# The modulation's products on VectorE alone, and layer 2's moved from the two input projections into the first FFN

## The chip, the cores and the metric

One core of one Trainium2 chip runs the kernel as one program. The metric is the device time of one execution in microseconds (us), lower is better. A run's time is compared by the median of several executions.

The engines that matter here are TensorE (PE), VectorE (DVE), ScalarE (ACT), GpSimd (POOL) and SyncE (SP), which issues most of the transfers. Each engine takes its instructions strictly in order, so an instruction that waits also holds up whatever stands behind it on the same engine.

## What is computed

Two layers of a hybrid backbone over 1024 latent and 128 context tokens, width 1024, everything in fp32:

```
for l in range(2):
    sh1, sc1, g1, sh2, sc2, g2 = split(silu(c) @ w_mod[l] + b_mod[l], 6)   # once for c, once for c_ctx
    u = rms_norm(x, norm1_g[l]) * (1 + sc1) + sh1
    mix = mixers(u @ w_in[l] + b_in[l])          # attention, gated DeltaNet, mLSTM
    x = x + g1 * (mix @ w_out[l])
    u = rms_norm(x, norm2_g[l]) * (1 + sc2) + sh2
    x = x + g2 * ((silu(u @ w_gate) * (u @ w_up)) @ w_down)
y = rms_norm(x, final_norm_g)
```

The change concerns the first line alone, the **modulation**: a vector of 1024 numbers (for each of two conditions) times a matrix of 1024 x 6144 per layer. The result is 48 blocks of 128 numbers per layer and condition. `sh1`, `sc1` and `g1` of a layer are needed around its mixers, `sh2`, `sc2` and `g2` around its FFN.

## The kernel before

Tokens lie along the free dimension in three groups of 384 (`GW`); features lie on the partitions in 8 blocks. Each fp32 product on PE is made of three matmuls with parts of the operands (`mm3`, lines 189 to 191): the weights are split by ACT (`wh`, line 183) and by DVE (`wl`, line 184).

A layer goes through these stages: `begin` and `w_in` (the input projection with the preparation of the mixers), `mixers` (recurrences and attention, then half 1 of the output projection), half 0 of `w_out`, the norm, and `ffn`. The emitted order is not the order in which engines run: a list scheduler puts each engine's instructions into a fixed order before the launch, and pools of buffers with a given number of copies (`bufs`) decide how far a producer may run ahead.

Blocks 0 to 15 of layer 1's modulation are made on PE at the very start (`adaln`). The other 80 are made by `ada`, while the input projections run: 32 of layer 1 and the first 16 of layer 2 in layer 1's `w_in`, the other 32 of layer 2 in layer 2's `w_in`. `ada_open` first loads the condition vectors onto every partition (`csb`, 1 MB) and lets ACT take the silu. For each block, 128 rows of the transposed weights (`aw`, 128 x 1024, 512 KB, 5 buffers) come in through SP's queue, and there are two ways to the sum of products along a row:

- condition 0 on DVE (line 240): one instruction multiplies and sums (`aj`), followed by a short readout of the accumulator;
- condition 1 on POOL and ACT: POOL multiplies (`ap`, line 243, 2 buffers), ACT sums (line 244).

In `w_in` up to 6 blocks of modulation are emitted behind each of the projection's blocks `b` from `LATE` = 1 on. The projection's own blocks need all engines too: `blk_b` (lines 700 to 716) multiplies on PE, moves the result out with ACT (`cv`, line 700) and convolves it on DVE (lines 704 to 708); `blk_c` (line 726) and `blk_a` (lines 912 to 952) do likewise.

In `ffn` one hidden block is a `gu` (two products `pg` and `pu`, 48 matmuls for each of three groups), after which DVE multiplies (`hs`, line 370) and splits (`hl`, line 203). Two hidden blocks then go through `dn`: 24 products `pd` of 6 matmuls, each added into `x` by DVE (`add_gated`, line 347). The banks `pg`, `pu` and `pd` have two buffers each in PSUM, and so has `st`, which only the norm uses.

## Time and profile before

| what | value |
|---|---|
| time, three runs | 3957.68, 3957.76 and 3968.36 us, median 3957.76 us |
| span of the profiled execution | 3963.4 us |
| its own time beside the span | not given apart; the span lies 5.6 us over the median |
| PE busy, share of the span | 3587.5 us, 91% |
| DVE busy | 2333.4 us, 59% |
| ACT busy | 1223.3 us, 31% |
| POOL busy | 904.9 us, 23% |
| mean granted clock of PE | 0.939 |

Busy shares are means over stages that differ. In the FFNs PE is busy all the time at its full clock and DVE about four tenths; in the input projections DVE is the fuller engine and PE has gaps. So the change has to be read stage by stage: layer 1's input projection lies within the first 640 us, the first FFN starts near 1200 us, and layer 2 starts near 2030 us.

### The profile page before, as it was taken

The page shows a single profiled execution, that of the slowest core. Times are in us where ns is not written, and L with a number is a line of the kernel's source. Part 1 is how long each engine was busy: PE and PEld are TensorE (multiplying, and loading weights), DVE is VectorE, ACT ScalarE, POOL GpSimd, SP SyncE. Part 2 cuts the span into 40 slices and gives each one's busy share as a digit, 9 for nine tenths or more (in the row PEclk, how much of TensorE's full clock was granted, in tenths as well). Part 3 has the DMA queues.
Part 4 walks back from the last instruction along what each step waited for, and adds up shares of the span by engine and source line. Part 5 has one row for each costly group of instructions (what it writes and reads, how often), then busy time and mean ns, then how long its engine had stood idle before and what let it go on. Part 6 is the DMA issues. An engine that isn't in the chain of part 4 may idle for free. (4 is left out here: it accounts for less than half of the span.)

```text
span 3963.4 us, 59219 instructions
## 1 busy us (share of the span) xinstructions
PE 3587.5 (91%) x22770; PEld 3417.7 (86%) x22770; DVE 2333.4 (59%) x5009; ACT 1223.3 (31%) x2544; POOL 904.9 (23%) x983
## 2 busy tenths in 40 slices
PE   7876888888899999999988798988889999999998
PEld 6876777788789999999987777878779999999997
DVE  7898575768654333333378957656785533433335
ACT  5343322535533111111143442233463411111111
POOL 2276340246310000000023735013551200000001
PEclk8988997899899999999998899979999999999999
DMA  5355743485411111111133575248652111111111
GB/s 206 129 197 165 241 159 111 118 242 155 149 54 38 38 49 43 38 43 43 40 121 135 192 246 182 90 114 246 175 160 68 38 43 38 44 47 38 38 49 59
DMA packets 270177, 434.11 MB, mean 110 GB/s; under 512 B 23880, under 2 KB 185736, under 8 KB 269640
## 3 DMA queue, kind: packets, MB, share of 16 engines
q1 hardware_dynamic: 240664, 324.28, 26.1%
q10 hardware_dynamic: 29232, 106.05, 8.4%
q8 instruction: 180, 2.95, 0.3%
q14 instruction: 101, 0.83, 0.1%
HBM read 315.85 MB, written 114.39 MB: 109 GB/s over the span
## 5 line engine op out<-in xcount | busy, mean ns | idle before, releaser
L347 DVE SCALAR_TENSOR_TENSOR x<-pd,mod,x 128x256 f32<-128x256 f32 (+1 forms) x832 | 404.1, 513 | 667.9 <-PE pd L191 667.2
L183 ACT CAST wh<-wr 128x1024 fp32r<-128x1024 f32 (+1 forms) x219 | 228.6, 1045 | 831.2 <-PE pu L190 457.6
L284 POOL TENSOR_TENSOR nacc<-nacc,nsq 128x384 f32<-128x384 f32 x48 | 52.0, 1083 | 1758.0 <-ACT nsq L283 1750.8
L189 PE MATMUL dn<-uh,wh 128*128 128x384 f32 x864 | 312.9, 362 | 82.7 <-ACT gw L726 37.7
L184 DVE TENSOR_TENSOR wl<-wr,wh 128x1024 fp32r<-128x1024 f32 (+1 forms) x219 | 279.9, 1287 | 164.1 <-ACT wh L183 163.6
L189 PE MATMUL pd<-hh,wh 128*128 128x384 f32 x1056 | 359.6, 341 | 6.9 <-DVE x L347 5.1
L190 PE MATMUL pg<-ul,wh 128*128 128x384 f32 x1056 | 357.9, 339 | 1.8 <-DVE ul L332 1.8
L189 PE MATMUL pg<-uh,wh 128*128 128x384 f32 x1056 | 356.0, 337 | 2.6 <-ACT uh L327 2.6
L190 PE MATMUL pd<-hl,wh 128*128 128x384 f32 x1056 | 356.2, 337 | 0.0
L191 PE MATMUL pd<-hh,wl 128*128 128x384 f32 x1056 | 355.9, 337 | 0.0
L189 PE MATMUL pu<-uh,wh 128*128 128x384 f32 x1056 | 355.3, 336 | 0.0
L190 PE MATMUL pu<-ul,wh 128*128 128x384 f32 x1056 | 355.3, 336 | 0.0
L191 PE MATMUL pg<-uh,wl 128*128 128x384 f32 x1056 | 353.1, 337 | 0.0
L191 PE MATMUL pu<-uh,wl 128*128 128x384 f32 x1056 | 349.1, 336 | 0.0
L190 PE MATMUL dn<-ul,wh 128*128 128x384 f32 x864 | 309.2, 358 | 0.0
L191 PE MATMUL dn<-uh,wl 128*128 128x384 f32 x864 | 307.8, 356 | 0.1
L243 POOL TENSOR_TENSOR ap<-aw,csb 128x1024 f32<-128x1024 f32 x80 | 253.2, 3191 | 220.9 <-ACT csb L229 147.0
L1232 PE MATMUL s<-K,Q 128*128 128x384 f32 (+1 forms) x800 | 229.1, 397 | 57.3 <-DMA Q<-QD 28.8
L189 PEld LDWEIGHTS dn<-uh,wh 128*128 128x128 f32 x864 | 175.1, 203 | 95.1 <-ACT gw L726 39.6
L1233 DVE TENSOR_SCALAR_CACHE_REDUCE e<-s 128x384 f32<-128x384 f32 (+1 forms) x400 | 209.8, 540 | 78.8 <-PE s L1232 73.2
L370 DVE TENSOR_TENSOR hs<-pu,hs 128x384 f32<-128x384 f32 x132 | 73.1, 554 | 239.8 <-PE pu L191 238.2
L189 PEld LDWEIGHTS pd<-hh,wh 128*128 128x128 f32 x1056 | 198.1, 188 | 15.8 <-issue 7.5
(354 smaller groups left out, 8650.3 us busy)
## 6 DMA issues: line engine op xcount, KB each, us to landing
wr<-in_w_gu_dram ACTq DMA_DIRECT2D x88, 512.0 KB
aw<-in_w_mod_dram SPq DMA_DIRECT2D x80, 512.0 KB
wr<-in_w_dn_dram ACTq DMA_DIRECT2D x44, 512.0 KB
wr<-in_w_st_dram ACTq DMA_DIRECT2D x36, 512.0 KB
rd<-RD SPq DMA_DIRECT2D x36, 512.0 KB
Q<-QD SPq DMA_DIRECT2D x64, 256.0 KB
RM<-em SPq DMA_DIRECT2D x36, 384.0 KB
rm<-RM SPq DMA_DIRECT2D x36, 384.0 KB
```

The source lines that it names most:

```text
L183: nc.scalar.copy(hi, r)
L184: (eng or nc.vector).tensor_tensor(out=lo, in0=r, in1=hi.bitcast(F32), op=ALU.subtract)
L189: mm(out, lhsT=wh, rhs=xh, start=start, stop=False)
L190: mm(out, lhsT=wh, rhs=xl, start=False, stop=False)
L191: mm(out, lhsT=wl, rhs=xh, start=False, stop=stop)
L243: nc.gpsimd.tensor_tensor(out=p, in0=w, in1=self.csb[:, i], op=ALU.mult)
L284: (nc.gpsimd if k in PST else nc.vector).tensor_tensor(out=self.acc[g], in0=self.acc[g], in1=s, op=ALU.add)
L347: nc.vector.scalar_tensor_tensor(out=x[g][k][:, lo:hi], in0=ps[:, lo:hi], scalar=gate[:, k, cnd:cnd + 1], in1=x[g][k][:, lo:hi], op0=ALU.m ...
L370: nc.vector.tensor_mul(s, pu[:, :GW], s)
L1232: nc.tensor.matmul(p[:, :w], lhsT=q[:, m, hl, 128 * j:128 * j + 128], rhs=K[m][:, 128 * ks[0]:128 * ks[0] + w], start=hl == 0, stop=hl == 1)
L1233: nc.vector.tensor_scalar(out=e[:, GW * i:GW * i + w], in0=p[:, :w], scalar1=0.125, scalar2=None, op0=ALU.mult, op1=ALU.max, accum_out=mx[ ...
```

## The change

Three things change.

1. In `ada` both conditions go the DVE way; POOL's multiply and ACT's sum are gone. `w_in` of layer 1 makes only layer 1's 32 blocks, `w_in` of layer 2 makes none and does not open `csb`.
2. All 48 blocks of layer 2 are made by `ada_halves` during layer 1's FFN: each block in two halves of 512 columns (`aw`, 256 KB, 3 buffers), two DVE instructions a half, whose unused product goes to the PSUM banks `st`. One half is emitted after each group of a `gu` from `b` = 2 on and after each `k` of a `dn`.
3. The pool of the norm (`nw`) is opened on the right side of SBUF for half 0 of `w_out`, closed before the FFN, where the buffers of `ada_halves` take its place, and opened again before the last `dn`.

```diff
-    def ada(self, l, b, pool, bufs, dve):
+    def ada(self, l, b, pool, bufs):
...
-        nc.sync.dma_start(w, self.A["w_mod1"][b] if l else self.A["w_mod0"][b - 16])
+        nc.sync.dma_start(w, self.A["w_mod0"][b - 16])
         for i in range(2):
             o = self.mod[l][:, b, i:i + 1]
-            if i in dve:
-                j = self.t(pool, [P, D], "aj", 1)
-                nc.vector.scalar_tensor_tensor(out=j, in0=w, scalar=1.0, in1=self.csb[:, i], op0=ALU.mult, op1=ALU.mult, accum_out=o)
-                continue
-            p = self.t(pool, [P, D], "ap", APB)
-            nc.gpsimd.tensor_tensor(out=p, in0=w, in1=self.csb[:, i], op=ALU.mult)
-            nc.scalar.activation(p, p, AF.Copy, accum_out=o)
+            j = self.t(pool, [P, D], "aj", 1)
+            nc.vector.scalar_tensor_tensor(out=j, in0=w, scalar=1.0, in1=self.csb[:, i], op0=ALU.mult, op1=ALU.mult, accum_out=o)
+
+    def ada_halves(self, l, pool, psp):
+
+        nc = self.nc
+        self.ada_open(pool)
+        part = pool.tile([P, 2, 48, 2], F32, name=self.nm("part"))
+        for b in range(48):
+            for h in range(2):
+                c = slice(512 * h, 512 * h + 512)
+                w = self.t(pool, [P, 512], "aw", 3)
+                nc.sync.dma_start(w, self.A["w_mod1"][b][:, c])
+                for i in range(2):
+                    j = self.ps(psp, "st", 2)
+                    nc.vector.scalar_tensor_tensor(out=j, in0=w, scalar=1.0, in1=self.csb[:, i, c], op0=ALU.mult, op1=ALU.mult,
+                                                   accum_out=part[:, h, b, i:i + 1])
+                yield
+        nc.vector.tensor_add(self.mod[l], part[:, 0], part[:, 1])
+        self.ada_bias(l, 0, 48)
...
                 nc.vector.tensor_mul(s, pu[:, :GW], s)
+                if b > 1:
+                    next(side, None)
...
                     for g in range(NG):
                         prod(W, bs, k, g)
+                    next(side, None)
                 return
-            # the last one by groups, with the norm that follows
+
+            last()
...
-                        for l1, jb in side[:n]:
-                            self.ada(l1, jb, sp, AWB, (0,))
+                        for jb in side[:n]:
+                            self.ada(l, jb, sp, AWB)
...
-                self.w_in(l, u, [(l, b) for b in range(16, 48)] + [(1, b) for b in range(16) if l == 0], *ps)
+                self.w_in(l, u, range(16, 48) if l == 0 else (), *ps)
...
-                nw = self.open_nw()
+                nw = self.open_nw("right")
...
+                    nw.close()
+                    ea = ExitStack()
+                    side = iter(())
+                    if l + 1 < LAY:
+                        side = self.ada_halves(l + 1, ea.enter_context(self.pool("adf", side="right")), pf)
...
+                    def last(side=side, ea=ea, reopened=reopened):
+                        for _ in side:
+                            pass
+                        ea.close()
+                        reopened.append(self.open_nw("right"))
```

The scheduler does not leave the half blocks where the code emits them. On DVE, where the weights of the third hidden block of the first FFN are split, the kernel before has this order (`hl`, `wl` and `hs` as above):

```order
L203 TENSOR_TENSOR hl_12385<-hs_12381,hh_12384 128x384
L184 TENSOR_TENSOR wl_12452<-wr_12453,wh_12451 128x1024
L370 TENSOR_TENSOR hs_12438<-pu_12413,hs_12438 128x384
L184 TENSOR_TENSOR wl_12629<-wr_12630,wh_12628 128x1024
L203 TENSOR_TENSOR hl_12442<-hs_12438,hh_12441 128x384
```

The changed kernel has at the same place (line 253 is the product of a half block, line 385 the `hs` of line 370 before):

```order
L203 TENSOR_TENSOR hl_12060<-hs_12056,hh_12059 128x384
L184 TENSOR_TENSOR wl_12127<-wr_12128,wh_12126 128x1024
L253 SCALAR_TENSOR_TENSOR st_12374,part_12371<-aw_12372,csb_12368 128x512
L253 SCALAR_TENSOR_TENSOR st_12376,part_12371<-aw_12372,csb_12368 128x512
L385 TENSOR_TENSOR hs_12113<-pu_12088,hs_12113 128x384
L253 SCALAR_TENSOR_TENSOR st_12437,part_12371<-aw_12435,csb_12368 128x512
L184 TENSOR_TENSOR wl_12304<-wr_12305,wh_12303 128x1024
L253 SCALAR_TENSOR_TENSOR st_12439,part_12371<-aw_12435,csb_12368 128x512
L203 TENSOR_TENSOR hl_12117<-hs_12113,hh_12116 128x384
```

The first half block stands ahead of work of hidden block 1 already, so the products begin earlier than the emitted `b` = 2. From there to the last of the 192 products, DVE has 93 instructions of the FFN between them: 13 `wl`, 15 `hs`, 13 `hl` and 52 additions into `x`. The last product stands just ahead of the fifteenth group of additions of the second `dn`. Inside the first `dn`, DVE's order in the changed kernel is (line 362 is the `add_gated` of line 347 before):

```order
L362 SCALAR_TENSOR_TENSOR x_1497_7795<-pd_12644,mod_73,x_1497_7795 128x384
L253 SCALAR_TENSOR_TENSOR st_14657,part_12371<-aw_14655,csb_12368 128x512
L253 SCALAR_TENSOR_TENSOR st_14659,part_12371<-aw_14655,csb_12368 128x512
L253 SCALAR_TENSOR_TENSOR st_14688,part_12371<-aw_14686,csb_12368 128x512
L253 SCALAR_TENSOR_TENSOR st_14690,part_12371<-aw_14686,csb_12368 128x512
L253 SCALAR_TENSOR_TENSOR st_14719,part_12371<-aw_14717,csb_12368 128x512
L362 SCALAR_TENSOR_TENSOR x_1505_7803<-pd_12652,mod_73,x_1505_7803 128x384
```

Before, two additions of this kind follow each other directly there. Now up to five products stand between them, and PE's bank `pd` comes free only behind them.

In layer 1's input projection, ACT's order before mixes the sums of condition 1 into the work of the projection (line 700 moves a product out of PSUM, line 707 belongs to the convolution):

```order
L244 ACTIVATE ap_1501,mod_73<-ap_1501 128x1024
L183 CAST wh_2239<-wr_2241 128x1024
L700 ACTIVATE cv_1821<-dn_1877,par_71 128x256
L700 ACTIVATE cv_1821<-dn_1877,par_71 128x128
L244 ACTIVATE ap_1508,mod_73<-ap_1508 128x1024
L707 ACTIVATE cv_1669<-cv_1752 128x1156
L244 ACTIVATE ap_1625,mod_73<-ap_1625 128x1024
```

In the changed kernel these sums are gone from that queue, and DVE's products of both conditions stand between its instructions of the convolution as those of one condition did before.

## Rows read from the trace of the kernel before

**Rows 1.** Stretches: length, busy us of each engine (instructions), PE's clock, DMA share, GB/s.

```profile
core 0: us, PE busy (x) PEld busy (x) DVE busy (x) ACT busy (x) POOL busy (x), PEclk, DMA share, GB/s
152.20:375.20 223.00, 150.87 (x760) 146.80 (x761) 209.51 (x165) 91.47 (x159) 164.19 (x61) 0.82 0.56 184
2123.60:2266.70 143.10, 102.27 (x528) 100.29 (x529) 135.92 (x102) 63.40 (x105) 104.20 (x33) 0.83 0.57 191
1211.00:1375.00 164.00, 164.00 (x945) 163.73 (x944) 54.83 (x94) 24.78 (x39) 0.00 (x0) 1.00 0.13 42
```

**Rows 2.** PE's waits, 140 to 420 us: us in total, times, longest.

```profile
PE dn L189 <- ACT gw L938: 33.2, 6, 9.0
PE dn L189 <- ACT gw L726: 18.7, 2, 12.4
PE pp L715 <- ACT cv L712: 16.7, 1, 16.7
```

**Rows 3.** DVE's groups, 152.2 to 375.2 us: busy us, mean ns | idle before.

```profile
L240 DVE SCALAR_TENSOR_TENSOR aj<-aw,csb 128x1024 f32<-128x1024 f32 x48 | 114.0, 2374 | 9.0 <-ACT csb L229 8.1 <-DMA aw<-in_w_mod_dram 0.4
L706 DVE SCALAR_TENSOR_TENSOR cv<-cv,cwh,cv 128x1156 f32<-128x1156 f32 x12 | 27.5, 2290 | 0.0
L184 DVE TENSOR_TENSOR wl<-wr,wh 128x1024 fp32r<-128x1024 f32 x9 | 19.7, 2185 | 0.0
```

**Rows 4.** DVE in order of time, layer 1's projection: start us, us, what.

```profile
181.36 3.42 DVE L240 SCALAR_TENSOR_TENSOR aj<-aw,csb 128x1024 f32<-128x1024 f32 x1
184.71 3.48 DVE L706 SCALAR_TENSOR_TENSOR cv<-cv,cwh,cv 128x1156 f32<-128x1156 f32 x1
188.12 1.21 DVE L240 SCALAR_TENSOR_TENSOR aj<-aw,csb 128x1024 f32<-128x1024 f32 x1
...
189.26 1.41 DVE L706 SCALAR_TENSOR_TENSOR cv<-cv,cwh,cv 128x1156 f32<-128x1156 f32 x1
...
269.59 1.21 DVE L240 SCALAR_TENSOR_TENSOR aj<-aw,csb 128x1024 f32<-128x1024 f32 x1
...
270.84 1.22 DVE L240 SCALAR_TENSOR_TENSOR aj<-aw,csb 128x1024 f32<-128x1024 f32 x1
```

**Rows 5.** POOL in order of time, same stretch; idle time before in brackets.

```profile
160.61 26.36 POOL L243 TENSOR_TENSOR ap<-aw,csb 128x1024 f32<-128x1024 f32 x8 [63.41 <-ACT csb L229]
195.47 9.61 POOL L243 TENSOR_TENSOR ap<-aw,csb 128x1024 f32<-128x1024 f32 x3 [8.49 <-ACT ap L244]
```

**Rows 6.** DVE in order of time: four landmarks, two in each layer.

```profile
152.22 0.18 DVE L716 COPY ss<-pp 128x18 f32<-128x18 f32 x1 [0.78 <-PE pp L715]
...
1194.23 0.54 DVE L370 TENSOR_TENSOR hs<-pu,hs 128x384 f32<-128x384 f32 x1
...
2123.63 0.18 DVE L716 COPY ss<-pp 128x18 f32<-128x18 f32 x1 [1.60 <-PE pp L715]
...
3115.87 0.54 DVE L370 TENSOR_TENSOR hs<-pu,hs 128x384 f32<-128x384 f32 x1
```

**Rows 7.** DVE's additions in the first FFN, by form, 1200 to 1900 us.

```profile
L347 DVE SCALAR_TENSOR_TENSOR x<-pd,mod,x 128x384 f32<-128x384 f32 x138 | 84.2, 615 | 182.5 <-PE pd L191 182.5
L347 DVE SCALAR_TENSOR_TENSOR x<-pd,mod,x 128x128 f32<-128x128 f32 x69 | 23.6, 342 | 0.0
```

**Rows 8.** SP's issue and ACT's silu of the condition vectors, in order of time.

```profile
151.78 0.38 SPq L228 DMA_DIRECT2D csb<-in_cB_dram  x1
...
158.57 1.91 ACT L229 ACTIVATE csb<-csb 128x2048 f32<-128x2048 f32 x1 [3.14 <-DMA csb<-in_cB_dram]
```

**Rows 9.** DVE in order of time, first FFN.

```profile
1211.45 0.55 DVE L370 TENSOR_TENSOR hs<-pu,hs 128x384 f32<-128x384 f32 x1
...
1367.73 0.62 DVE L347 SCALAR_TENSOR_TENSOR x<-pd,mod,x 128x384 f32<-128x384 f32 x1 [2.96 <-PE pd L191]
...
1372.95 0.74 DVE L347 SCALAR_TENSOR_TENSOR x<-pd,mod,x 128x256 f32<-128x256 f32 x2 [2.75 <-PE pd L191]
```

**Rows 10.** A load of 512 KB: SP's issue, and POOL that waits for it.

```profile
239.95 2.81 SPq L235 DMA_DIRECT2D aw<-in_w_mod_dram  x2
...
243.52 2.39 POOL L243 TENSOR_TENSOR ap<-aw,csb 128x1024 f32<-128x1024 f32 x1 [5.99 <-DMA aw<-in_w_mod_dram]
```

More of the change, by code (lines that the diff above doesn't have):

```diff
@@ L229, in ada_open @@
         self.nc.scalar.activation(self.csb, self.csb, AF.Silu)
[L231 removed]
+    def ada(self, l, b, pool, bufs):
         nc = self.nc
         w = self.t(pool, [P, D], "aw", bufs)
[L235 removed]
+        nc.sync.dma_start(w, self.A["w_mod0"][b - 16])
         for i in range(2):
             o = self.mod[l][:, b, i:i + 1]
[L238 to L244 removed]
+            j = self.t(pool, [P, D], "aj", 1)
[16 more added lines that the diff above has]
+        self.ada_bias(l, 0, 48)
+        self.ada_scale(l, self.a1[l], "n1g", 8)
+        self.ada_scale(l, self.a2[l], "n2g", 32)
     def ada_bias(self, l, b0, b1):
@@ L352, in gu_w, with ffn @@
         return [self.load_w(self.A["w_gu"][l, 2 * b + i]) for i in range(2)]
-    def ffn(self, l, x, u, hp, psp, before, norm):
+    def ffn(self, l, x, u, hp, psp, before, norm, side, last):
         nc, A = self.nc, self.A
@@ L457, in w_in @@
             with self.pool("side", side="right") as sp:
-                self.ada_open(sp)
+                if side:
+                    self.ada_open(sp)
                 n = -(-len(side) // (10 - LATE))
@@ L467, in w_in @@
                     if b >= LATE:
-                        for l1, jb in side[:n]:
-                            self.ada(l1, jb, sp, AWB, (0,))
+                        for jb in side[:n]:
+                            self.ada(l, jb, sp, AWB)
                         side = side[n:]
-                self.ada_bias(l, 16, 48)
-                self.ada_scale(l, self.a2[l], "n2g", 32)
                 if l == 0:
-                    self.ada_bias(1, 0, 16)
-                    self.ada_scale(1, self.a1[1], "n1g", 8)
+                    self.ada_bias(l, 16, 48)
+                    self.ada_scale(l, self.a2[l], "n2g", 32)
             ch = self.ch = es.enter_context(self.pool("chunk", side="right"))
@@ L1368, in run, with before @@
                     u = [list(self.norm_g(x, self.a2[l], self.mod[l][:, 24:32, :], g, self.rstd(g, pf))) for g in range(NG)]
-                    with self.pool("ffn") as hp:
-                        def before(l=l):
-                            if l + 1 < LAY:
-                                self.pre = self.cvg_w(l + 1)
-                        if l + 1 < LAY:
-                            norm = lambda g, R, x=x, l=l: self.norm_g(x, self.a1[l + 1], self.mod[l + 1][:, 0:8, :], g, R)
-                        else:
-                            norm = lambda g, R, x=x: self.norm_y(x, g, R)
-                        u = self.ffn(l, x, u, hp, pf, before, norm)
-                        if l + 1 == LAY:
-                            list(norm(2, self.rstd(2, pf, "st", 2, "pg")))
+                    nw.close()
[3 more added lines that the diff above has]
+                        side = self.ada_halves(l + 1, ea.enter_context(self.pool("adf", side="right")), pf)
+                        norm = lambda g, R, x=x, l=l: self.norm_g(x, self.a1[l + 1], self.mod[l + 1][:, 0:8, :], g, R)
+                    else:
+                        norm = lambda g, R, x=x: self.norm_y(x, g, R)
+                    reopened = []
+                    def last(side=side, ea=ea, reopened=reopened):
[3 more added lines that the diff above has]
+                        reopened.append(self.open_nw("right"))
+                    def before(l=l):
+                        if l + 1 < LAY:
+                            self.pre = self.cvg_w(l + 1)
+                    with self.pool("ffn") as hp:
+                        u = self.ffn(l, x, u, hp, pf, before, norm, side, last)
+                    nw = reopened[0]
+                    if l + 1 == LAY:
+                        list(norm(2, self.rstd(2, pf, "st", 2, "pg")))
                 if l + 1 < LAY:
```

## The prediction

> **What bounds the kernel now.** I read the windows by stage first, because the busy shares of the whole span mix stages that have nothing in common. In the stretch of layer 1's projection in which the modulation runs, 223.0 us long, DVE is busy for 209.5 us, PE for only 150.9 us, and PE's granted clock is 0.82, a mix of its two levels 1.2 and 2.4 GHz. Layer 2's stretch is the same picture in 143.1 us, and in the first FFN it is reversed: PE 164.0 of 164.0 us at clock 1.00, DVE 54.8 us [rows 1]. So the modulation lengthens the projections through DVE, and in the FFN DVE has room.
>
> The chain of waits shows how it reaches PE. PE waits there for ACT, which moves results out of PSUM: 33.2, 18.7 and 16.7 us are the largest entries [rows 2]. ACT in turn stands in order behind its sums of POOL's products and behind DVE.
>
> The groups by line and the order of time show why DVE is full. A product of 1024 columns takes 2374 ns in the mean, a convolution step of 1156 columns 2290 ns, a split 2185 ns [rows 3]. Yet these are means of two prices. While POOL multiplies without a break, from 160.6 to 187.0 us, DVE's product takes 3.42 us and the convolution step 3.48 us; from 187.0 until POOL starts again at 195.5 us the same two take 1.21 and 1.41 us [rows 4, 5]. POOL's multiply of two SBUF operands triples DVE's instructions. That is the price which this change removes.
>
> **Layer 1's projection.** Removed: 48 multiplies on POOL and 48 sums on ACT. DVE has 48 products now and 64 after. Their undisturbed price is read between starts: 1.14 us when another operation follows (188.12 to 189.26) and 1.25 us when another product follows, with the accumulator's readout between (269.59 to 270.84) [rows 4]. I take 1.20 us, so 64 products are 77 us in place of 114.0 us and some 4 us of readouts. DVE's other work is 209.5 - 114.0 - 4 = 92 us. Of this the convolution steps fall from 27.5 us to 12 x 1.41 = 17 us and the splits from 19.7 us to 9 x 1.21 = 11 us, a factor of 0.59; the other 45 us by the same factor become 27 us [rows 3, 4]. Together 55 us. DVE's wait of 8.1 us for the condition vectors stays [rows 3]. The sum for DVE is 77 + 55 + 8 = 140 us, against 209.5 + 8.1 = 218 us: 78 us less. PE cannot be faster than its matmuls: in the FFN 945 of them go through in 164.00 us, 0.174 us each, so 760 take 132 us [rows 1]. Both floors lie near 140 us. Two full engines that wait for each other do not run at their floors, so I take 67 of the 78 us; bounds 40 (half of it) and 80 (PE's floor leaves 91, DVE's saving is less).
>
> **Layer 2's projection.** All 32 blocks go, on every engine, and so do the transfer of `csb`, its silu and 32 transfers of 512 KB in SP's queue, behind which the projection's own stores stand. DVE no longer bounds. PE's floor is 528 x 0.174 = 92 us of 143.1 us, so at most 51 us can come back [rows 1]. I take 44 us, which leaves 7 us for the convolution's chain from DVE over ACT to PE's short products; lower bound 35.
>
> That time won here reaches later stages can be read from the two layers, which do the same work with 48 and 32 blocks. From the copy of the norms of the keys to the first hidden block of the FFN, layer 1 takes 1194.23 - 152.22 = 1042.0 us, layer 2 takes 3115.87 - 2123.63 = 992.2 us [rows 6]. Sixteen blocks cost 49.8 us at the far end, 3.1 us each.
>
> **The first FFN.** Added: 192 products of 512 columns on DVE, 96 loads of 256 KB, one load of `csb` and its silu. No row shows such a product or a DVE instruction that writes PSUM. Its price: the additions take 615 ns at 384 columns and 342 ns at 128, so a column costs 1.07 ns and 512 columns 0.545 us [rows 7]. From 1.14 and 1.25 us between starts this leaves 0.60 and 0.71 us. Most products have another product behind them, so I take 0.69 us, 132 us in all. Lower bound 0.60, 115 us. Upper bound: the additions, which touch PSUM, have a fixed part of 615 - 410 = 205 ns, the full product in SBUF 1210 - 1090 = 120 ns; if the difference of 85 ns comes on top of 0.71 us, 0.79 us, 152 us [rows 4, 7].
>
> The Trainium skill, on the page Perfetto Trace Analysis, section Optimizing Scalar/DVE Operations, gives DVE about 60 ns of access overhead on SBUF and about 125 ns on PSUM. Taken in full that would be an estimated 65 ns x 192 = 12 us more, and the forecast 3887 instead of 3875. The trace agrees with the direction, by the two fixed parts of 120 and 205 ns [rows 4, 7], and cannot split it between reading and writing.
>
> The order decides how much of this PE sees. The products are not spread over the FFN: all 192 stand between hidden block 1 and the second `dn`, from 1211 us to the addition that starts at 1372.95 us [rows 9], about the window of 164 us. DVE's load there becomes 54.8 + 132 = 187 us, 23 us more than there is [rows 1]. DVE also starts late: `csb` can only be loaded when the norm has left its buffers, and takes 158.57 + 1.91 - 151.78 = 8.7 us from issue to the end of its silu [rows 8], of which about 5 us fall behind the first product's place. At the start that is hidden by the second banks of `pg` and `pu`; it adds to the debt. At the end PE can lend some: an addition at 1367.73 us frees a bank whose next product is added at 1372.95 us, after about 1 us of matmuls, 4 us of slack [rows 9]. So PE loses 23 + 5 - 4 = 24 us, behind `add_gated`, `hs` and `wl`. I add 2 us for loads that land late: a load of 512 KB was used 3.6 us after its issue (239.95 to 243.52) [rows 10]; with three buffers a half block then needs (3.6 + 0.4 + 1.4) / 3 = 1.8 us, just under the 187 / 96 = 1.95 us that DVE takes for it. Cost 26 us, bounds 9 and 50.
>
> **Half 0 of the output projection.** On the right side, the norm's first buffers lie where half 1 kept its operands, so the first load waits for PE. One late load is worth at most the 3.6 us above a layer; most of it passes while half 1 still multiplies. I take 2 us in all, bounds 0 and 8. Opening and closing the pool later costs nothing: those buffers are long free.
>
> **The sum.** 67 + 44 - 26 - 2 = 83 us. The profiled execution's span of 3963.4 us becomes 3880 us. It lies 5.6 us over the median of the three runs, 3957.8 us, and a microsecond saved in the one is taken as one in the other: 3875 us.
>
> **Rivals.**
> - DVE stays the bound in layer 1. The products stand ahead of convolution steps in its queue, and 64 of them are more than 48. If only 40 us come back: 3957.8 - 40 - 44 + 28 = 3902 us. For it speaks that both floors are equal; against it that DVE has 78 us less to do.
> - The half blocks starve on their three buffers (slower). If a load needs L us from release to landing, 96 half blocks take 96 x (L + 1.4) / 3. The 111 us won are lost, but for the 2 us of the output projection, when the stretch of 164 us becomes 273 us, at L = 7.1 us. At L = 8 us it is 301 us, and the time 3957.8 - 111 + 137 + 2 = 3986 us. Against it speak the 3.6 us of a load twice as large at DMA share 0.56, and the share of 0.13 in the FFN [rows 1, 10].
> - The gains of the projections are eaten on the way to the FFN, since what follows is bound otherwise, and a third arrives: 3957.8 - 37 + 28 = 3949 us, no change. Against it stands the 49.8 us between the layers [rows 6].
> - The 2374 ns are the product's own price and POOL is innocent (slower). Then layer 1 pays 16 x 2.37 = 38 us more on DVE, and the FFN 192 x 1.19 = 228 us in place of 132, 122 us with the rest: 3957.8 + 38 - 44 + 122 + 2 = 4076 us. The 1.21 us with POOL idle speak against it [rows 4, 5]. It is the way to which a rule of the Trainium skill points, Perfetto Trace Analysis, Optimizing Scalar/DVE Operations: where DVE is saturated, handing some of its work to ScalarE or GpSimd may pay. This change takes the work back to a DVE that is saturated. The same section doubts such a move between DVE and GpSimd, and the rows side with the doubt.
>
> **How the numbers follow.** Forecast 0.73, layer 1 still bound 0.15, starving 0.05, nothing arrives 0.05, POOL innocent 0.02. The time is the forecast's, 3875 us. The extremes of its terms are 80 + 51 - 9 - 0 = 122 us won, 3836 us, and 40 + 35 - 50 - 8 = 17 us won, 3941 us; this range also holds the first rival and leaves out about 0.12. What a measurement here can tell from no change is 0.3%, 12 us. Faster: the forecast, the first rival and a little of the third, 0.89. Same: most of the third, 0.03. Slower: the rest, 0.08.
>
> **What would show it.** Right: DVE's products near 1.21 us and convolution steps near 1.41 us throughout; the two stretches near 156 and 99 us; PE's clock above 0.9 in them; in the FFN half products of about 0.66 us, and about 25 us of waits of PE for line 362 and its neighbours before the end of the second `dn`, none after. Wrong: products that still take 3.4 us with POOL idle; DVE waiting for `aw` in the FFN for tens of us; PE's clock falling in the FFN, which I priced at nothing beyond the waits; or a reordering by the scheduler that opens new gaps in the mixers, which I cannot see from here.

## The result and the profile after

| kernel | runs | time, median (range) | ratio, 95% interval |
|---|---|---|---|
| before | 4 | 3961.14 us (3957.68 to 3968.36) | |
| after | 4 | 3807.75 us (3804.74 to 3813.90) | 0.9619 [0.9604, 0.9633] |

The change makes the kernel 153 us faster. The forecast was 83 us, with a low end of 3836 us, so direction and mechanism were right and the size was not. The profiled execution of after took 3805.75 us around a span of 3804.0 us; its span is 159.4 us shorter than that of before.

The page of the kernel after, busy time by engine:

```profile
PE 3543.6 (93%) x22770; PEld 3370.6 (89%) x22770; DVE 2278.1 (60%) x5361; ACT 1136.1 (30%) x2383; POOL 651.2 (17%) x903
```

POOL lost 254 us of work and DVE, which took it over, is busy for 55 us less than before. Before, then, part of DVE's busy time was not work of its own: its instructions took longer than they need.

The same stretches as in [rows 1], by windows of the kernel after: layer 1's modulation (its second `ss` to the last product), the stretch behind it up to the last product of the projection that has the features on the partitions (`dn<-uh,wh` on PE), a piece of layer 2's projection, and the 192 half products in the first FFN.

```profile
core 0: us, PE busy (x) PEld busy (x) DVE busy (x) ACT busy (x) POOL busy (x), PEclk, DMA share, GB/s
153.00:299.20 146.20, 141.08 (x813) 140.00 (x814) 132.72 (x199) 45.41 (x69) 22.14 (x17) 0.99 0.69 231
299.20:383.90 84.70, 81.54 (x405) 65.91 (x405) 52.04 (x100) 34.92 (x100) 30.16 (x52) 0.90 0.76 255
2033.30:2120.00 86.70, 86.70 (x506) 86.60 (x505) 33.28 (x42) 24.73 (x38) 0.00 (x0) 0.98 0.33 111
1108.30:1287.50 179.20, 167.70 (x936) 162.72 (x936) 173.23 (x476) 26.41 (x41) 0.00 (x0) 0.99 0.55 175
```

In layer 1 PE now does 813 matmuls in 146.2 us, where it did 760 in 223.0 us, and in layer 2 it has no gap at all. The granted clock rose from 0.82 and 0.83 to 0.99 and 0.98.

The stretch behind layer 1's modulation of before, and the last products `dn<-uh,wh` of layers 1 and 2, first of before, then of after (first and last start in us):

```profile
375.20:482.60 107.40, 95.82 (x463) 79.30 (x462) 58.88 (x111) 41.40 (x115) 38.92 (x64) 0.92 0.73 233
```

```profile
L189 PE MATMUL dn<-uh,wh x345: 332/336/689, 152.3 to 482.3; 128*128 128x384 f32 x173
...
L189 PE MATMUL dn<-uh,wh x345: 331/336/689, 2123.9 to 2432.3; 128*128 128x384 f32 x173
```

```profile
L189 PE MATMUL dn<-uh,wh x345: 332/336/689, 153.3 to 383.6; 128*128 128x384 f32 x173
...
L189 PE MATMUL dn<-uh,wh x345: 331/336/687, 2034.3 to 2288.2; 128*128 128x384 f32 x173
```

PE's waits from 140 to 420 us, the two largest, against 33.2, 18.7 and 16.7 us in [rows 2]:

```profile
PE dn L189 <- ACT gw L956: 4.4, 3, 2.9
PE pp L771 <- DMA c<-CQK: 3.7, 2, 2.8
```

DVE's groups in layer 1's stretch of after, the lines that answer to [rows 3]:

```profile
L239 DVE SCALAR_TENSOR_TENSOR aj<-aw,csb 128x1024 f32<-128x1024 f32 x64 | 84.1, 1314 | 8.4 <-ACT csb L229 7.5
L724 DVE SCALAR_TENSOR_TENSOR cv<-cv,cwh,cv 128x1156 f32<-128x1156 f32 x12 | 17.0, 1418 | 0.0
L184 DVE TENSOR_TENSOR wl<-wr,wh 128x1024 fp32r<-128x1024 f32 x10 | 12.7, 1274 | 2.9 <-ACT wh L183 2.9
```

The convolution step fell from 2290 to 1418 ns, the split from 2185 to 1274 ns.

The landmarks of [rows 6] in after, DVE in order of time:

```profile
152.96 0.18 DVE L734 COPY ss<-pp 128x18 f32<-128x18 f32 x1 [2.11 <-PE pp L733]
...
1088.31 0.54 DVE L385 TENSOR_TENSOR hs<-pu,hs 128x384 f32<-128x384 f32 x1
...
2033.99 0.18 DVE L734 COPY ss<-pp 128x18 f32<-128x18 f32 x1 [2.24 <-PE pp L733]
...
2961.66 0.55 DVE L385 TENSOR_TENSOR hs<-pu,hs 128x384 f32<-128x384 f32 x1
```

They split the 159.4 us. Layer 1 up to its FFN takes 935.3 us instead of 1042.0 (107 us won), layer 2 takes 927.7 instead of 992.2 (65 us won). The first FFN, from its first `hs` to its last addition, takes 845.6 instead of 829.7 us (16 us lost). The second FFN, from its first to its last `hs`, takes 791.4 instead of 796.5 us (5 us won). What is left is about 1 us.

The last two come from these rows, the additions of the first FFN and the hidden products of the second, by tile, with the first and the last start in us; first of after, then of before:

```profile
L362 DVE SCALAR_TENSOR_TENSOR x<-pd,mod,x x352: 332/546/620, 1159.7 to 1933.9; 128x384 f32<-128x384 f32 x88, 128x256 f32<-128x256 f32 x88
...
L385 DVE TENSOR_TENSOR hs<-pu,hs x66: 544/557/558, 2961.7 to 3753.1; 128x384 f32<-128x384 f32 x66
```

```profile
L347 DVE SCALAR_TENSOR_TENSOR x<-pd,mod,x x352: 333/546/620, 1261.5 to 2023.9; 128x384 f32<-128x384 f32 x88, 128x256 f32<-128x256 f32 x88
...
L370 DVE TENSOR_TENSOR hs<-pu,hs x66: 543/557/559, 3115.9 to 3912.4; 128x384 f32<-128x384 f32 x66
```

### The profile page after: what moved, and what is told of

It is laid out like the page before. It is cut to its first block, busy times and chain, and to the rows that moved or that the text cites. A ratio compares the mean times of both kernels' runs of the same rounds, so it can differ in the third digit from the quotient of the medians.

```text
span 3804.0 us, 59431 instructions
## 1 busy us (share of the span) xinstructions
PE 3543.6 (93%) x22770; PEld 3370.6 (89%) x22770; DVE 2278.1 (60%) x5361; ACT 1136.1 (30%) x2383; POOL 651.2 (17%) x903
## 5 line engine op out<-in xcount | busy, mean ns | idle before, releaser
L184 DVE TENSOR_TENSOR wl<-wr,wh 128x1024 fp32r<-128x1024 f32 (+1 forms) x219 | 267.2, 1229 | 176.5 <-ACT wh L183 175.9
L189 PE MATMUL dn<-uh,wh 128*128 128x384 f32 x864 | 299.3, 346 | 5.1 <-ACT gw L956 4.4
L190 PE MATMUL dn<-ul,wh 128*128 128x384 f32 x864 | 298.1, 345 | 0.0
L191 PE MATMUL dn<-uh,wl 128*128 128x384 f32 x864 | 297.6, 344 | 0.1
L1250 PEld LDWEIGHTS s<-K,Q 128*128 128x128 f32 x800 | 136.9, 205 | 82.4 <-DVE e L1251 41.2
L189 PE MATMUL dn<-wh,uh 128*128 128x256 f32 (+1 forms) x624 | 185.9, 298 | 24.5 <-DVE gw L558 19.0
L191 PEld LDWEIGHTS pg<-uh,wl 128*128 128x128 f32 x1056 | 199.6, 189 | 9.0 <-DVE wl L184 6.6
```

The costliest lines, as they stand in the source:

```text
L184: (eng or nc.vector).tensor_tensor(out=lo, in0=r, in1=hi.bitcast(F32), op=ALU.subtract)
L189: mm(out, lhsT=wh, rhs=xh, start=start, stop=False)
L190: mm(out, lhsT=wh, rhs=xl, start=False, stop=False)
L191: mm(out, lhsT=wl, rhs=xh, start=False, stop=stop)
L1250: nc.tensor.matmul(p[:, :w], lhsT=q[:, m, hl, 128 * j:128 * j + 128], rhs=K[m][:, 128 * ks[0]:128 * ks[0] + w], start=hl == 0, stop=hl == 1)
```

## The experiments

All runs in one table. The columns are the median time, the ratio to the kernel before with its interval, and the stretches between the landmarks above in each kernel's trace.

| kernel | us | ratio | layer 1 | FFN 1 | layer 2 | FFN 2 |
|---|---|---|---|---|---|---|
| before | 3961.14 | | 1042.0 | 829.7 | 992.2 | 796.5 |
| after | 3807.75 | 0.9619 [0.9604, 0.9633] | 935.3 | 845.6 | 927.7 | 791.4 |
| dve_in_place | 3899.89 | 0.9847 [0.9822, 0.9871] | 1001.4 | 829.7 | 963.0 | 796.7 |
| pool_layer1 | 3862.26 | 0.9740 [0.9715, 0.9764] | 998.9 | 845.6 | 928.7 | 791.5 |
| pool_extra_two | 3872.31 | 0.9785 [0.9766, 0.9805] | 1002.2 | 847.9 | 927.8 | 791.5 |
| pool_extra_one | 3864.37 | 0.9765 [0.9745, 0.9785] | 1010.1 | 845.5 | 917.6 | 791.4 |
| no_l1_products | 3804.15 | 0.9602 [0.9573, 0.9631] | 942.1 | 845.0 | 920.6 | 791.8 |
| no_ffn_products | 3803.35 | 0.9592 [0.9572, 0.9611] | 943.7 | 828.4 | 936.9 | 791.5 |
| two_buffers | 3822.39 | 0.9651 [0.9625, 0.9676] | 940.5 | 861.8 | 927.3 | 791.5 |
| sbuf_dest | 3793.75 | 0.9582 [0.9557, 0.9607] | 933.2 | 831.6 | 927.4 | 791.7 |
| spread | 3824.86 | 0.9652 [0.9626, 0.9677] | 943.3 | 857.7 | 935.8 | 791.5 |
| spread3 | 3789.62 | 0.9570 [0.9543, 0.9597] | 941.5 | 835.9 | 924.2 | 781.4 |
| nw_right | 3952.00 | 0.9983 [0.9972, 0.9994] | 1031.5 | 828.5 | 985.3 | 791.4 |

Kernels that share the code of a stretch show how far one can trust it. Layer 1 is the same in after, no_ffn_products, two_buffers, sbuf_dest, spread and spread3, and takes 933 to 944 us: a difference of less than 10 us there says nothing. Layer 2 has no modulation in after and in all kernels derived from it, and takes 918 to 937 us: there up to 20 us say nothing. The first FFN is the same in after, pool_layer1, pool_extra_one, no_l1_products and pool_extra_two, and takes 845.0 to 845.6 us in the first four and 847.9 in the last: there more than 3 us count.

### Is it POOL that makes DVE slow?

**dve_in_place**, on the kernel before:

```diff
-                            self.ada(l1, jb, sp, AWB, (0,))
+                            self.ada(l1, jb, sp, AWB, (0, 1))
```

> The kernel before with one edit: both conditions go the DVE way, all 80 blocks stay in the two input projections, and POOL multiplies nothing there. Theory (POOL's multiplies slow DVE): DVE's products take about 1.2 us, so layer 1's stretch holds 96 x 1.2 = 115 us of products, 55 of other work and 8 of waiting, 178 us in place of 223, and layer 2's about 77 + 34 + 8 = 119 in place of 143. With some more won right behind the two stretches, as between before and after, 70 to 90 us in all: 3870 to 3890 us. Rival (POOL is innocent, a product costs 2.37 us): 48 + 32 more products cost 80 x 2.37 = 190 us, 4150 us. Second rival (only the place of the work matters): no gain, 3961 us.

Measured: 3899.89 us, 10 us above the theory's range and far from both rivals. DVE makes 80 more products and the kernel is 1.5% faster; layer 1 wins 41 us and layer 2 29 us. The theory's stretches of 178 and 119 us did not come out: up to the last product they took 242.4 and 143.0 us, because other work had moved into them (PE did 1200 and 788 matmuls there, in place of 760 and 528).

**pool_layer1**, on the changed kernel: in `ada`, condition 1 goes to POOL and ACT again.

```diff
+            p = self.t(pool, [P, D], "ap", APB)
+            nc.gpsimd.tensor_tensor(out=p, in0=w, in1=self.csb[:, i], op=ALU.mult)
+            nc.scalar.activation(p, p, AF.Copy, accum_out=o)
```

> The changed kernel with one edit: in layer 1's projection condition 1 of its 32 blocks goes back to POOL and ACT, layer 2's half blocks stay in the FFN. DVE has 32 products there in place of 64. Theory (POOL's multiplies slow DVE): products and convolution steps take above 3 us while POOL runs, and layer 1 gives back about 16 blocks' worth less than before had lost, 330 - 231 - 50 = 50 us: 3858 us. Rival (the gain came from moving the 16 blocks of layer 2 away): DVE has less to do than in the changed kernel, 3808 us or less.

Measured: 3862.26 us, as the theory had it. Halving DVE's products costs layer 1 64 us.

**pool_extra_two**, on the changed kernel: a multiply on POOL for each block of layer 1, whose result nobody reads.

```diff
+        p = self.t(pool, [P, D], "ap", APB)
+        nc.gpsimd.tensor_tensor(out=p, in0=w, in1=self.csb[:, 1], op=ALU.mult)
```

> The changed kernel with one addition: for each of layer 1's 32 blocks POOL also multiplies the block by the second condition vector (two SBUF operands, 128 x 1024), into a buffer that nobody reads. DVE still makes all 64 products. It measures the disputed price by itself: nothing depends on POOL's result. Theory (POOL's multiply slows whatever DVE does meanwhile): products and convolution steps take above 3 us while POOL runs, POOL needs about 3.4 us for each of its 32, so for some 110 us DVE works at a third of its speed; layer 1 grows by 50 to 70 us, 3860 to 3880 us. Rival (the slow products of before came from the scheduler's order or from the loads): 3808 us, products at 1.2 us.

Measured: 3872.31 us, and layer 1 takes 1002 us, within 4 us of pool_layer1. POOL's 32 multiplies cost 60 to 70 us, whether or not anything depends on them. DVE and POOL of this kernel in order of time:

```profile
158.82 1.22 DVE L239 SCALAR_TENSOR_TENSOR aj<-aw,csb 128x1024 f32<-128x1024 f32 x1 [7.39 <-ACT csb L229]
...
160.09 3.30 DVE L239 SCALAR_TENSOR_TENSOR aj<-aw,csb 128x1024 f32<-128x1024 f32 x1
...
163.32 3.41 DVE L184 TENSOR_TENSOR wl<-wr,wh 128x1024 fp32r<-128x1024 f32 x1
...
179.67 1.21 DVE L239 SCALAR_TENSOR_TENSOR aj<-aw,csb 128x1024 f32<-128x1024 f32 x1
```

```profile
158.92 19.61 POOL L241 TENSOR_TENSOR ap<-aw,csb 128x1024 f32<-128x1024 f32 x6 [63.48 <-ACT csb L229]
180.06 3.02 POOL L241 TENSOR_TENSOR ap<-aw,csb 128x1024 f32<-128x1024 f32 x1 [1.53 <-DMA aw<-in_w_mod_dram]
```

The product that starts 0.1 us ahead of POOL takes 1.22 us. Those behind it take 3.3 to 3.4 us, one for each of POOL's six (19.61 / 6 = 3.27 us). When POOL waits for its next block, at 178.5 us, the product is back at 1.21 us.

The Trainium skill, SBUF — State Buffer, section Who interferes with whom, states that a DVE instruction with two SBUF inputs contends with a GpSimd instruction that reads SBUF, and that the ports which they share are an exclusive lock. The rows above agree: 3.30 us beside POOL's 3.27 us.

**pool_extra_one**: the same with one SBUF operand.

```diff
+        nc.gpsimd.tensor_scalar(out=p, in0=w, scalar1=0.5, scalar2=None, op0=ALU.mult)
```

> As pool_extra_two, but POOL multiplies the block by a constant: one SBUF operand in place of two, the same 128 x 1024 elements read and written. Theory (it is the second SBUF operand that makes POOL and DVE take turns): products stay at 1.2 us, 3808 us. Rival (any POOL instruction on SBUF slows DVE in proportion to the data it moves): products above 1.2 us in the mean, and a time between 3815 us and that of pool_extra_two.

Measured: 3864.37 us. For DVE's products the rival holds, in part: their mean in this stretch is 1502 ns, against 1856 ns in pool_extra_two and 1314 ns in after. DVE and POOL in order of time:

```profile
172.01 2.18 DVE L726 SCALAR_TENSOR_TENSOR cv<-cv,cwh,cv 128x1156 f32<-128x1156 f32 x1
174.12 1.21 DVE L239 SCALAR_TENSOR_TENSOR aj<-aw,csb 128x1024 f32<-128x1024 f32 x1
...
175.26 2.18 DVE L726 SCALAR_TENSOR_TENSOR cv<-cv,cwh,cv 128x1156 f32<-128x1156 f32 x1
```

```profile
159.59 24.87 POOL L241 TENSOR_SCALAR ap<-aw 128x1024 f32<-128x1024 f32 x8 [63.56 <-DMA aw<-in_w_mod_dram]
```

POOL still needs 3.1 us for each, without a break, but DVE does a product at full speed and a convolution step that is 0.77 us late (2.18 in place of 1.41) in that time. So one operand holds DVE up by about 0.8 us for each instruction of POOL, two by about 2.1. The time did not fall by as much: it lies in the rival's range, and layer 1 takes 1010 us. Three windows show where the two kernels lose, each from the second `ss` over about 800 matmuls: after, pool_extra_two and pool_extra_one.

```profile
153.00:294.00 141.00, 138.82 (x802) 138.06 (x803) 127.53 (x189) 42.86 (x65) 21.16 (x15) 0.99 0.69 234
```

```profile
151.20:358.00 206.80, 153.09 (x799) 149.86 (x799) 194.02 (x191) 42.51 (x66) 118.73 (x48) 0.87 0.49 163
```

```profile
153.90:329.00 175.10, 148.47 (x802) 144.63 (x803) 155.96 (x207) 45.29 (x73) 125.61 (x51) 0.90 0.59 196
```

With two operands this work takes 66 us more, nearly all that layer 1 loses, and DVE is busy for 66 us more with two instructions more: there the price is DVE's slower instructions. With one operand it takes 34 us more, and DVE is busy for 28 us more, with 18 instructions more. The other 41 us of layer 1's loss come behind this stretch. There POOL's own part of the projection stands in order behind the added instructions; whether that makes these 41 us is not shown.

### What do layer 1's 32 blocks still cost?

**no_l1_products**, on the changed kernel:

```diff
-                self.w_in(l, u, range(16, 48) if l == 0 else (), *ps)
+                self.w_in(l, u, (), *ps)
...
+                    nc.vector.memset(self.mod[l][:, 16:48, :], 0.0)
```

> The changed kernel without layer 1's 32 blocks: no load of the condition vectors, no loads and no products in layer 1's projection; those columns of the modulation are set to zero before bias and scale, so that part of the computation is left out. It measures what 32 blocks on DVE alone still cost layer 1. Theory from the landmarks (layer 1 from the norms of the keys to the first hidden product 938 us, layer 2 without any modulation 930 to 939 us): almost nothing, 0 to 10 us, 3798 to 3808 us. Rival (as the prediction had it, the stretch stays above PE's floor by 156 - 132 = 24 us): 3784 us.

Measured: 3804.15 us, no difference from after that can be measured. The window that answers to layer 1's stretch:

```profile
153.60:299.00 145.40, 145.40 (x829) 134.97 (x830) 69.21 (x110) 53.71 (x121) 21.94 (x40) 0.99 0.52 172
```

Without a single product PE does 829 matmuls in 145.4 us; with all 64 it does 813 in 146.2. The sixty-four products of DVE cost PE about 16 matmuls, some 3 us, which layer 1 as a whole does not show (942.1 us without them, 935.3 with them). dve_in_place has 32 more of them there, and layer 1 takes 57 to 66 us more. This is not a price of 2 us for each product, as its windows beside those of after show, each from the second `ss` over the first 2000 matmuls and over the next 400; first after, then dve_in_place:

```profile
153.00:512.00 359.00, 337.68 (x1999) 306.00 (x2000) 279.33 (x505) 108.36 (x250) 101.68 (x168) 0.94 0.63 213
512.00:549.00 37.00, 34.20 (x402) 31.91 (x400) 24.29 (x62) 8.29 (x28) 0.00 (x0) 1.00 0.23 72
```

```profile
154.80:512.80 358.00, 329.80 (x2004) 306.50 (x2004) 272.31 (x452) 104.03 (x234) 69.10 (x101) 0.95 0.67 227
512.80:615.80 103.00, 67.15 (x399) 52.47 (x398) 96.46 (x260) 27.79 (x71) 43.65 (x78) 0.77 0.36 103
```

Up to matmul 2000, more than 100 us behind the last product, the two are level. The next 400 take 103.0 us in place of 37.0, with DVE busy for 96.5 of them: DVE's other work was pushed behind the products, and there it bounds. Nor does the number of products alone decide: in layer 2 of dve_in_place 64 of them cost 26 to 45 us (963.0 against 918 to 937 without any), where in layer 1 of after 64 cost nothing.

### What does the first FFN cost, and why?

**no_ffn_products**, on the changed kernel: `ada_halves` without its loads and products.

```diff
-        self.ada_open(pool)
...
-        nc.vector.tensor_add(self.mod[l], part[:, 0], part[:, 1])
+        yield
+        nc.vector.memset(self.mod[l], 0.0)
```

> The changed kernel without layer 2's products: no load of the condition vectors, no half blocks and no readouts in the first FFN; layer 2's modulation is set to zero before bias and scale, so that part of the computation is left out. All else stays. Theory from the landmarks (first hidden product to last addition: 829.7 us before, 845.6 after): the FFN's cost is 16 us, so 3792 us. The prediction's term of 26 us would give 3782 us. Rival (the 16 us are a difference between executions): 3808 us. The mixers and the second FFN, which came out 17 and 5 us shorter than in the trace of before, stay as in the changed kernel if that comes from the changed order, and differ by some us if executions differ.

Measured: the first FFN takes 828.4 us, 17.2 less than in after. The whole time is 3803.35 us, 11 us above the theory's and only 4 us below after (by the ratios 11). In the profiled execution layers 1 and 2 took 8 and 9 us more than in that of after; the code of layer 1 is the same, so this is within what executions differ by.

**two_buffers**, on the changed kernel:

```diff
-                w = self.t(pool, [P, 512], "aw", 3)
+                w = self.t(pool, [P, 512], "aw", 2)
```

> The changed kernel with one edit: 2 buffers in place of 3 for the half blocks. The prediction's rule for starving, 96 x (L + 1.4) / buffers with L = 3.6 us from release to landing, gives 160 us for 3 buffers (below the 179 us that the products took) and 240 us for 2: the stretch and the time grow by about 60 us, 3868 us, with DVE idle for aw by about as much. Rival (a half block lands faster than L = 2.3 us, or PE has slack for the waits): no change, 3808 us.

Measured: the products take 226.8 us in place of 179.2, and DVE waits for `aw` 34.6 us. So the rule came near (226.8 x 2 / 96 - 1.3 = 3.4 us for a load in place of 3.6, with 1.3 us for the two products), but the FFN grew by 16 us, not by 60.

**sbuf_dest**, on the changed kernel:

```diff
-                    j = self.ps(psp, "st", 2)
+                    j = self.t(pool, [P, 512], "aj", 1)
```

> The changed kernel with one edit: the unused half product goes to a buffer in SBUF (one copy) and not to the PSUM banks st. In the trace of the changed kernel two half products stand 0.65 us apart with PSUM as target; in the kernel spread, with SBUF as target, 0.73 us. Theory (PSUM is the cheaper target here, since the readout of the accumulator then lies under the next instruction): 0.08 x 192 = 15 us more for DVE in a stretch where DVE is full, so the first FFN grows by 10 to 15 us, 3820 us. Rival (writing to PSUM costs more than to SBUF, as the larger fixed part of the additions suggested): DVE saves up to 12 us, 3796 us.

Measured: 3793.75 us and a first FFN of 831.6 us. The theory fell. The rival's time came true, but not by its reason, since with this target the products take DVE longer. In order of time, half products in after and then in sbuf_dest:

```profile
1129.18 0.69 DVE L253 SCALAR_TENSOR_TENSOR st<-aw,csb 128x512 f32<-128x512 f32 x1
1129.79 0.14 DVE L253 DVE_READ_ACCUMULATOR st<-aw,csb 128x1 f32 x1
1129.79 0.73 DVE L253 SCALAR_TENSOR_TENSOR st<-aw,csb 128x512 f32<-128x512 f32 x1
1130.43 0.14 DVE L253 DVE_READ_ACCUMULATOR st<-aw,csb 128x1 f32 x1
1130.43 0.73 DVE L253 SCALAR_TENSOR_TENSOR st<-aw,csb 128x512 f32<-128x512 f32 x1
```

```profile
1117.33 0.69 DVE L253 SCALAR_TENSOR_TENSOR aj<-aw,csb 128x512 f32<-128x512 f32 x1
1117.95 0.08 DVE L253 DVE_READ_ACCUMULATOR aj<-aw,csb 128x1 f32 x1
1118.07 0.69 DVE L253 SCALAR_TENSOR_TENSOR aj<-aw,csb 128x512 f32<-128x512 f32 x1
```

Into PSUM the next product starts 0.61 to 0.65 us after the last, together with the readout; in sbuf_dest it starts 0.73 us after, 0.12 us behind the readout's start. That is not the price of SBUF as the target. `st` has two buffers and `aj` here has one. In spread3 (below) the target is SBUF with three buffers, and there products follow each other like this:

```profile
1161.50 0.68 DVE L253 SCALAR_TENSOR_TENSOR hs<-aw,csb 128x512 f32<-128x512 f32 x1
...
1162.10 0.68 DVE L253 SCALAR_TENSOR_TENSOR hs<-aw,csb 128x512 f32<-128x512 f32 x1
...
1162.72 0.68 DVE L253 SCALAR_TENSOR_TENSOR hs<-aw,csb 128x512 f32<-128x512 f32 x1
```

They are 0.60 to 0.62 us apart, below the 0.64 to 0.65 us into PSUM. Where one product directly follows another, it starts within 0.64 us in 45 of 102 cases in spread3, in 30 of 102 in spread with two buffers, and in none of 111 in sbuf_dest with one. So the 0.12 us most likely are a wait for a free buffer; no run changed the number of buffers of `aj` alone. DVE has more to do in sbuf_dest, and yet PE waits less. The likely reason is the order, as three windows show: sbuf_dest and two_buffers from the first to the last half product, and no_ffn_products over the part of the FFN that after, sbuf_dest and two_buffers get through in that time.

```profile
1107.50:1315.90 208.40, 208.26 (x1194) 205.89 (x1193) 195.92 (x507) 35.38 (x57) 0.00 (x0) 1.00 0.51 163
```

```profile
1110.90:1337.70 226.80, 208.43 (x1119) 201.72 (x1118) 188.30 (x497) 33.26 (x54) 0.00 (x0) 0.95 0.46 146
```

```profile
1115.20:1277.20 162.00, 162.00 (x935) 161.70 (x935) 52.24 (x90) 23.82 (x37) 0.00 (x0) 1.00 0.12 40
1115.20:1321.20 206.00, 206.00 (x1188) 205.41 (x1188) 70.67 (x121) 33.25 (x52) 0.00 (x0) 1.00 0.13 44
1114.50:1307.80 193.30, 193.30 (x1115) 192.71 (x1114) 65.80 (x114) 31.48 (x50) 0.00 (x0) 1.00 0.13 43
```

In the three kernels with products the stretch is made of the FFN's own work on DVE, the products, and DVE's idle time, which is small, but for the 34.6 us that two_buffers waits for `aw`. In after that is 52 + 121 + 6 = 179 us, in sbuf_dest 71 + 125 + 12 = 208 us, in two_buffers 66 + 122 + 39 = 227 us (the products are what the busy time leaves). What PE loses is this length less the time that PE's own work of the same stretch needs: 179 - 162 = 17 us, 208 - 206 = 2 us, 227 - 193 = 34 us. Only a part of it is gaps: in after PE is busy for 167.7 us with 936 matmuls where 935 take 162.0 us without the products, so 5.7 of the 17 us are slower matmuls, at a granted clock of 0.99; in two_buffers it is about 15 of the 34 us, at 0.95. And how much of the FFN lies in the stretch is fixed before the launch by DVE's order: between the first and the last product stand some 90 instructions of the FFN in after, 124 in sbuf_dest and 114 in two_buffers. That the scheduler chose another order because of the target is read from the orders; no run had SBUF as target with after's order.

**spread** and **spread3**, on the changed kernel. The half blocks are emitted with the hidden products alone, and their result goes into the ring of `hs`, of 2 buffers or of 3:

```diff
-                    j = self.ps(psp, "st", 2)
+                    j = self.t(hp, [P, 512], "hs", 2)
...
                 if b > 1:
-                    next(side, None)
+                    for _ in range(2 if (3 * b + g) % 5 in (0, 2, 4) else 1):
+                        next(side, None)
...
-                    next(side, None)
                 return
```

> The changed kernel with the half blocks spread over the whole first FFN: the unused product goes into the ring of buffers of the hidden blocks (hs, SBUF), so that a half block can't run ahead of the hidden product in front of which it is emitted; one or two half blocks for each hidden product from the third hidden block on, none for a dn. Theory (the FFN pays because 187 us of DVE work were crowded into 165 to 180 us): with DVE at about half load PE hardly waits, 10 to 14 us come back, 3796 us. Rival (every product in front of an hs or an addition delays PE, crowded or not): no change, 3808 us. Second rival (the ring ties products to the splits and starts new waits): slower than 3808 us.

> The kernel spread with 3 buffers in the ring of hidden products and half products in place of 2. In spread, ACT's silu waited for half products to leave the ring, the splits of the weights behind it came late, and the first FFN took 857.7 us against 845.6. Theory (the ring is to blame, not the spreading): with a third buffer ACT waits less and the first FFN falls below 850 us, 3800 to 3812 us. Rival (each half product in front of an addition or a split costs PE some 0.15 us, crowded or not): 857 us again, 3825 us.

Measured: spread 3824.86 us with a first FFN of 857.7 us, worse than after, and spread3 3789.62 us with 835.9 us. The one is what the second rival said; the other lies 10 us below the theory's range, with the FFN where the theory had it. A third buffer in the ring took 22 us off. ACT's silu, which writes into the ring, waited for DVE for 75.6 us in spread and 32.7 us in spread3, as the theory said; that this is the whole of the 22 us is not shown. spread3 and sbuf_dest are both faster than the changed kernel, by intervals that meet its own barely or not at all, and by a first FFN that is 10 and 14 us shorter where more than 3 us count. sbuf_dest comes within 3 us of the FFN without any products. Between the two the runs don't decide; spread3 also changes the second FFN, where `hs` has three buffers too (10 us less up to its last `hs`, 8 us more behind it).

### The norm's pool by itself

**nw_right**, on the kernel before:

```diff
-                nw = self.open_nw()
+                nw = self.open_nw("right")
```

> The kernel before with the third part of the change alone, in its simplest form: the norm's pool opened on the right side of SBUF for half 0 of the output projection, kept open through the FFN; the modulation stays on DVE, POOL and ACT in the projections. The prediction's term for this part is 2 us lost, bounds 0 and 8: 3963 us. Second question: the second FFN takes 796.5 us from first to last hidden product in both kernels with the pool on the left, and 791.4 to 791.8 us in the kernels derived from the changed one with a ring of two. Theory (where the buffers lie makes the 5 us): 791.5 us here. Rival (something else of the change does): 796.5 us.

Measured: 3952.00 us, 0.17% faster with an interval that excludes no change, and the second FFN takes 791.4 us. All kernels with the pool on the left have 796.5 or 796.7 us there, all with it on the right and two buffers for `hs` 791.4 to 791.8. So the place of the buffers, not the modulation, makes these 5 us. By which mechanism stays open.

## Why the prediction was right about the way and wrong about the size

- **POOL's price: right.** Products at 1.22 us (the median of 64) and convolution steps at 1.42 us came as forecast, and pool_extra_two shows the price alone. Eight products still took 1.76 to 2.04 us, each beside an instruction of two SBUF operands that POOL does for the projection itself. The rival "POOL is innocent" is gone.
- **Layer 1: 67 us forecast, 107 us measured.** Here the prediction failed. DVE's sum was 140 us and came out so (132.7 busy and 7.5 waiting), in part by luck: the products took 85 us with their readouts in place of 77, the other work 48 in place of 55. The step that failed is "Two full engines that wait for each other do not run at their floors, so I take 67 of the 78 us", with its upper bound from DVE's saving. First, they did run near their floors: PE was busy for 141.1 of 146.2 us, and the stretch became 77 us shorter, 10 more than forecast and within the bounds. Second, and this is the larger part, the stretch was cut where the modulation ends, and the saving in it was taken for the layer's gain. But PE did 813 matmuls in it in place of 760; at that pace 760 take 137 us, 86 us less than before. Behind the stretch there was less left to do, 405 matmuls in place of 463, and it took 84.7 us in place of 107.4. Up to the last `dn<-uh,wh` layer 1 took 330.1 us before and 230.6 after, 100 us won; the remaining 7 us are within what executions differ by. no_l1_products confirms it from the other side: nothing is left to win.
- **Layer 2: 44 us forecast, 65 measured, above the bound of 51.** The floor of 92 us for 528 matmuls was right: 506 went through in 86.7 us without a gap, so the 7 us left for the convolution's chain were not needed. That gives 53 us. Up to the last `dn<-uh,wh` it is 54.5 us (308.7 before, 254.2 after), and another 10 us come behind, within what executions differ by. So the reserve of 7 us failed; that the bound was wrong as well is not shown.
- **[rows 6] said more than the prediction took from it.** They priced 16 blocks at 49.8 us, of which layer 1 loses 16 and layer 2 loses 32. pool_layer1 measures the 16 leaving layer 1 alone at 43 us, and then POOL's leaving at 64 us. The prediction used the rows only to say that gains arrive.
- **The FFN: 26 us forecast, 17.2 measured.** DVE was the fuller engine as forecast, and one term was mis-sized: 0.69 us for a half product. DVE was busy for 121 us with 192 of them, 0.63 us each. The prediction's own sum with 0.63 is 54.8 + 121 - 164 = 12, and 12 + 5 - 4 + 2 = 15 us. That this comes so near 17.2 is partly luck, since the sum is one of waits, and 5.7 us of the loss are slower matmuls, which the prediction had put at nothing.
- **The overhead of PSUM** that the prediction cites (the Trainium skill, Perfetto Trace Analysis, Optimizing Scalar/DVE Operations) would have made each half product an estimated 65 ns dearer than into SBUF. The rows agree with the direction and not with the size: 0.64 to 0.65 us from start to start into PSUM, 0.60 to 0.62 us into SBUF with three buffers.
- **Half 0 of the output projection: 2 us lost forecast.** nw_right wins about 7 us in all, 5 of them in the second FFN; no loss shows.
- **The rival "DVE stays the bound in layer 1"** is refuted by no_l1_products: without any product the kernel is no faster.
- **The rival of the starving buffers** priced the stretch rightly and the loss wrongly: a longer stretch is lost to PE only by what the order does not fill with work of the FFN.

The misses add up: 42 us in layer 1 (half 0 among them), 21 in layer 2, 10 in the first FFN and 5 in the second are 78 us, where the spans differ by 159 - 83 = 76 us.

## What to carry to other kernels

Where an instruction's mean mixes two prices, look for the other engine that runs during the dear ones; taking 80 multiplies from POOL won more time than the 80 products that DVE got in return cost. When a stretch is relieved, don't cap the gain at the saving of its fullest engine inside the stretch: take the work that was pushed behind it to the next landmark, and take from twin stages with more and less of the load what a unit costs end to end. For work tucked into a stage that another engine bounds, and for as long as it fills its own engine there, the loss is the filler engine's total time less the bounding engine's time over the stretch that the order spans, so look at letting the order span more before making the filler cheaper. More span alone is no gain: spread spans most of the FFN and loses 29 us, of which a third buffer in its ring gives 22 back.

## What the runs showed of the hardware

- While POOL multiplies two SBUF operands of 128 x 1024, DVE instructions of two SBUF operands take 3.3 to 3.5 us in place of 1.2 to 1.4, one for each of POOL's. With one SBUF operand POOL is as slow (3.1 us) but delays DVE by only about 0.8 us. The exclusive lock of the Trainium skill's page SBUF — State Buffer, section Who interferes with whom, fits the first and not the second.
- A DVE product with accumulated sum has a readout behind it. Into PSUM (512 columns, two banks) the readout takes 0.14 us and the next product starts with it, 0.61 to 0.65 us after the last. Into SBUF the readout takes 0.08 us; the next product starts 0.73 us after the last with one buffer to write to (sbuf_dest), and 0.60 to 0.62 us after in 45 of 102 cases with a ring of three (spread3).
- The second FFN's 66 hidden products take 791.4 or 796.5 us for the same instructions, by where the norm's buffers lie (nw_right and before).
